# One address difference of activations and weights, modulo 256 bytes, in all products of a two-layer decoder trunk

## The chip, the cores and the metric

The kernel runs on one core of one Trainium2 chip. The metric is the device time of one execution in microseconds (us). The kernel before took 1021.05 us in the median of three runs (1021.05, 1022.01 and 1016.73). One further execution was profiled.

## What is computed

Two decoder layers over 256 tokens with a width of 1024, all in float32. The reference, cut to what matters here:

```python
for layer in range(2):
    if layer == 1:
        k_sh, v_sh, F_sh = shared_kv(x, c_act, ...)      # keys, values, forget gates, once
    sh1, sc1, g1, sh2, sc2, g2, sh3, sc3, g3 = split(c_act @ ada_w[layer] + ada_b[layer], 9)
    h = rms_norm(x, norm_g[layer, 0]) * (1 + sc1) + sh1
    x = x + 0.5 * g1 * swiglu(h, ffn_w_in[layer, 0], ffn_w_out[layer, 0])
    h = rms_norm(x, norm_g[layer, 1]) * (1 + sc2) + sh2
    x = x + g2 * (diff_attention(h, ...) if layer == 0 else forgetting_attention(h, ...))
    h = rms_norm(x, norm_g[layer, 2]) * (1 + sc3) + sh3
    x = x + 0.5 * g3 * swiglu(h, ffn_w_in[layer, 1], ffn_w_out[layer, 1])
return rms_norm(x, final_g)
```

`swiglu(h, w_in, w_out)` is `(silu(g) * u) @ w_out` with `g, u = split(h @ w_in)`; the hidden width is 2816. The four feed-forward networks (FFNs) are named (layer, place) here: (0,0), (0,1), (1,0), (1,1). They hold most of the work.

## The kernel before

**Products.** Activations lie transposed: 8 blocks `k` of 128 channels by 256 tokens. Each float32 operand is split into a high part in the format fp32r and the rest, and a product is made of three matmuls, `wh*xh`, `wl*xh` and `wh*xl` (`mm3`, line 391). Each has a 128x128 block of weights as its stationary operand, which is loaded with an instruction of its own, and 256 columns of activations as its moving operand (258 in the stages called "late", below). Each weight load runs beside the matmul ahead of it. In the products with the values' weights (`v_proj`) the roles are exchanged.

**Where the operands lie.** `HH` and `HL` (lines 399 and 400) hold the high and low parts of the normed activations, 8 blocks of `SP_` = 288 columns, 1152 bytes apart. `hidh` and `hidl` hold those of the hidden layer of an FFN, 512 columns each. Weights come in pieces of up to 1024 columns: `raw` from HBM, `wh` made of it by ScalarE (ACT; `cp_part`, line 281), and `wl` by VectorE (DVE; `sub_part`, line 291), in pools of 6, 6 and 5 buffers. Blocks within a piece are 512 bytes apart.

**Stages.** An FFN has input products into PSUM tiles `pg` and `pu` (gate and up; `pf` in the first stage of FFN (0,0), `lg` and `lu` in the first stage of (0,1) and (1,1)), eleven groups `j` of 96 matmuls, `k` the outer loop in each, and then output products into `po`, 8 tiles of 66 matmuls. Between the FFNs stand the differential attention (0) with its output projection `pw`, the shared keys and values, and the forgetting attention (1). A stage is called "late" where its first products run on activations that are not yet divided by their root mean square: that factor `r` comes from a matmul `psn` with a matrix of equal entries over the sum of squares `acc` (all but the last) and the last square `sq` (`rstd_of`, line 441), while the products `lp` or `lg` run on; then `make_h` (line 456) writes the true `HH` and `HL` block by block with a buffer `ht` between its three steps (DVE, ACT, DVE). The shared keys begin so: `lp` for the first two tiles of keys (`late_pairs`, line 491), then `pk` for the others, from the new `HH` and `HL`, then `pzf`, the forget gates, from weights `fg`, which ACT and DVE split into `fgh` and `fgl` (lines 986 to 999).

**What sets the order.** Instructions of TensorE (PE), ACT, DVE and the DMA queue of SyncE (SP) stay in the order in which the program names them; a planner (`InOrder`, `fill_act`, `fill_dve`, `bg`) puts the conversions of weights between the others by costs of its own. Instructions that the program gives directly to GpSimd (POOL), the DMA of `fg` among them, are placed by the scheduler of the tile framework. A tile with a tag takes the next buffer of its pool's tag and has to wait until the last reader of the tile that held it is done.

Of the kernel before, what the change touches and what calls it, by code (L numbers as in the profile page):

```python
# [10 lines left out]
F32 = mybir.dt.float32  # L11
F32R = mybir.dt.float32r
# [20 lines left out]
SX = S + 2  # L33
SP_ = 288
CP_SLACK = 0.3
# [71 lines left out]
def trunk(ctx, tc, a, out):  # L107
# [45 lines left out]
    cact = cp_.tile([P, D], F32, name="cact")  # L153
    small = cp_.tile([P, 32], F32, name="small")
    nmods = [0]
# [82 lines left out]
    def add_ffn(l, i):  # L238
        if (l, i) == (0, 0):
# [18 lines left out]
    pieces = [(src, c0, min(step, ncols - c0), c0 + step >= ncols)  # L258
              for src, ncols, step in stream for c0 in range(0, ncols, step)]
    raws, his, los = [], [], []  # L260
    taken = [0]
# [19 lines left out]
    def cp_part():  # L281

        u = len(his)
        n = pieces[u][2]
        act.t = max(act.t, used[u - NHI] if u >= NHI else 0.0)
        raw = raws[u]
        wh = wp.tile([P, 1024], F32R, tag="wh", name="wh")
        act.plainly(lambda: act.copy(wh[:, :n], raw[:, :n]))
        his.append(wh)

    def sub_part():
# [5 lines left out]
        dve.t = max(dve.t, used[u - NLO] if u >= NLO else 0.0)  # L297
        wl = wp.tile([P, 1024], F32R, tag="wl", name="wl", bufs=NLO)
        dve.plainly(lambda: dve.tensor_tensor(wl[:, :n], raws[u][:, :n], his[u][:, :n].bitcast(F32),
# [112 lines left out]
    def x_update(n, ps, gate, nxt, acc_eng):  # L412
# [14 lines left out]
        def second():  # L427
# [5 lines left out]
            elif n < NC - 1:  # L433
                t = kp.tile([P, S], F32, tag="acc", name=f"acc{n}")
                acc_eng.tensor_tensor(t, acc[0], sq, op=ALU.add)
# [20 lines left out]
    def make_h(k, r, m):  # L456

        A, sh = mods[m[0]][1], mods[m[1]][0]
        t = kp.tile([P, S], F32, tag="ht", name=f"ht{k}", bufs=3)
        dve.scalar_tensor_tensor(t, x[k], A[:, k:k + 1], r, op0=ALU.mult, op1=ALU.mult)  # L460
# [30 lines left out]
    def late_pairs(src, dsts, m, then):  # L491
# [5 lines left out]
        def out(i):  # L497
            c = late_cols(pb[i])
            for b in range(2):
                t = kp.tile([P, S], F32, tag="lt", name="lt")  # L500
                dve.tensor_tensor(t, pb[i][b][:, :S], r, op=ALU.mult)
# [23 lines left out]
    def ffn(l, i, kind, m, nxt, at=2):  # L525
# [56 lines left out]
        elif kind == "late":  # L582
# [19 lines left out]
            def late_out(b):  # L602
                if b == 0:
                    cols.append(late_cols(banks))
                c = cols[0]
                t = kp.tile([P, S], F32, tag="lt", name=f"lt{b}")
                dve.tensor_tensor(t, banks[b][:, :S], r, op=ALU.mult)
# [377 lines left out]
    vb = [[cp_.tile([P, 512], F32, name=f"vb{t}{nh}") for nh in range(2)] for t in range(2)]  # L985
    fg = kp.tile([P, NC, BH], F32, tag="fg", name="fg", bufs=1)
    nc.gpsimd.dma_start(fg, a["fgw"])
# [313 lines left out]
```

## Time and profile before

| | |
|---|---|
| runs, median (lowest to highest) | 1021.05 us (1016.73 to 1022.01) |
| profiled execution, its own time | 1017.31 us |
| its span in the trace | 1015.4 us |
| PE, matmuls | 991.7 us busy, 8076 matmuls |
| PE, weight loads | 953.8 us busy |
| DVE | 820.2 us busy |
| ACT | 563.5 us busy |
| DMA | 265.06 MB, 261 GB/s in the mean |

The span runs from the first to the last instruction of the program; 1.9 us of the execution's own time lie around it. Matmuls are pipelined: the busy time of one overlaps the next, so the pace of a stream of matmuls is read from start to start, not from the duration of one.

### The profile page before, as it was taken

The page shows a single profiled execution, that of the slowest core. Times are in us where ns is not written, and L with a number is a line of the kernel's source. Part 1 is how long each engine was busy: PE and PEld are TensorE (multiplying, and loading weights), DVE is VectorE, ACT ScalarE, POOL GpSimd, SP SyncE. Part 2 cuts the span into 40 slices and gives each one's busy share as a digit, 9 for nine tenths or more (in the row PEclk, how much of TensorE's full clock was granted, in tenths as well). Part 3 has the DMA queues.
Part 4 walks back from the last instruction along what each step waited for, and adds up shares of the span by engine and source line. Part 5 has one row for each costly group of instructions (what it writes and reads, how often), then busy time and mean ns, then how long its engine had stood idle before and what let it go on. Part 6 is the DMA issues. An engine that isn't in the chain of part 4 may idle for free.

```text
span 1015.4 us, 20397 instructions
## 1 busy us (share of the span) xinstructions
PE 991.7 (98%) x8076; PEld 953.8 (94%) x8076; DVE 820.2 (81%) x1379; ACT 563.5 (55%) x922; POOL 38.1 (4%) x64
## 2 busy tenths in 40 slices
PE   5999999999999999999999999999999999999996
PEld 4999999988899999999998999999987799999996
DVE  6989879899889998878898888889887788555553
ACT  4365545576777645455666444454575575444552
POOL 0000100001111000000000000000011010000000
PEclk9999999999999999999999999999999999999999
DMA  9988999969666799788867999888854337655661
GB/s 348 415 323 281 328 364 340 349 213 339 189 218 214 261 382 338 277 278 309 303 241 262 339 322 349 316 287 323 265 150 124 104 126 238 193 190 148 170 184 42
DMA packets 68129, 265.06 MB, mean 261 GB/s; under 512 B 7961, under 2 KB 8113, under 8 KB 57922
## 3 DMA queue, kind: packets, MB, share of 16 engines
q1 hardware_dynamic: 65810, 258.31, 72.4%
q0 software_dynamic: 1792, 4.81, 1.8%
q8 instruction: 63, 1.03, 0.4%
q10 hardware_dynamic: 432, 0.64, 0.2%
q14 instruction: 32, 0.26, 0.1%
HBM read 262.66 MB, written 2.65 MB: 261 GB/s over the span
## 4 chain that ended last, share of the span: by engine, by line
PE 90%; ACT 3%; DMA 2%; DVE 2%; issue 1%; POOL 1%; SPq 0%; DVEq 0%; ACTq 0%; POOLq 0%
PE po L102 23%; PE pg L102 21%; PE pu L102 21%; PE pf L102 5%; PE pv L102 4%; PE lp L102 3%; PE pw L102 3%; PE pqk L102 1%; ACT nl L102 1%; PE pob L102 1%; PE lg L102 1%; PE lu L102 1%; PE pk L102 1%; PE sb L102 1%; DMA ada<-in_ada 1%
## 5 line engine op out<-in xcount | busy, mean ns | idle before, releaser
L102 DVE TENSOR_TENSOR wl<-raw,wh 128x1024 fp32r<-128x1024 f32 (+1 forms) x368 | 401.7, 1105 | 98.4 <-issue 27.4
L102 ACT CAST wh<-raw 128x1024 fp32r<-128x1024 f32 (+1 forms) x368 | 349.7, 958 | 218.4 <-PE pu L102 107.2
L102 DVE CUSTOM_DVE_ANT_0 ada<-ada,cact,vecs 128x1024 f32<-128x1024 f32 x160 | 203.6, 1279 | 0.0
L102 PE MATMUL po<-hidh,wl 128*128 128x256 f32 x704 | 195.2, 277 | 0.0
L102 PE MATMUL po<-hidl,wh 128*128 128x256 f32 x704 | 195.2, 277 | 0.0
L102 PE MATMUL po<-hidh,wh 128*128 128x256 f32 x704 | 195.2, 277 | 0.0
L102 PE MATMUL pg<-HH,wl 128*128 128x256 f32 x608 | 169.8, 279 | 0.0
L102 PE MATMUL pg<-HH,wh 128*128 128x256 f32 x608 | 169.5, 279 | 0.0
L102 PE MATMUL pg<-HL,wh 128*128 128x256 f32 x608 | 169.4, 279 | 0.0
L102 PE MATMUL pu<-HH,wl 128*128 128x256 f32 x608 | 169.4, 279 | 0.0
L102 PE MATMUL pu<-HH,wh 128*128 128x256 f32 x608 | 169.2, 278 | 0.0
L102 PE MATMUL pu<-HL,wh 128*128 128x256 f32 x608 | 169.2, 278 | 0.0
L102 PEld LDWEIGHTS po<-hidl,wh 128*128 128x128 f32 x704 | 132.9, 189 | 0.0
L102 PEld LDWEIGHTS po<-hidh,wh 128*128 128x128 f32 x704 | 132.2, 188 | 0.0
L102 PEld LDWEIGHTS po<-hidh,wl 128*128 128x128 f32 x704 | 132.2, 188 | 0.0
L102 PEld LDWEIGHTS pg<-HH,wh 128*128 128x128 f32 x608 | 114.2, 188 | 0.7 <-issue 0.6
L102 PEld LDWEIGHTS pu<-HL,wh 128*128 128x128 f32 x608 | 114.4, 188 | 0.0
L102 PEld LDWEIGHTS pg<-HL,wh 128*128 128x128 f32 x608 | 114.2, 188 | 0.0
L102 PEld LDWEIGHTS pu<-HH,wh 128*128 128x128 f32 x608 | 114.2, 188 | 0.0
L102 PEld LDWEIGHTS pg<-HH,wl 128*128 128x128 f32 x608 | 114.1, 188 | 0.0
L102 PEld LDWEIGHTS pu<-HH,wl 128*128 128x128 f32 x608 | 114.1, 188 | 0.0
L102 ACT CAST hidh<-hf 128x512 fp32r<-128x512 f32 x44 | 27.3, 620 | 40.1 <-DVE hf L102 39.9
(204 smaller groups left out, 1603.7 us busy)
## 6 DMA issues: line engine op xcount, KB each, us to landing
raw<-in_win SPq DMA_DIRECT2D x176, 512.0 KB, 5.7
ada<-in_ada SPq DMA_DIRECT2D x79, 1024.0 KB, 7.3
raw<-in_wout SPq DMA_DIRECT2D x64, 384.0 KB, 5.0
raw<-in_wout SPq DMA_DIRECT2D x64, 320.0 KB, 4.4
raw<-in_wqk SPq DMA_DIRECT2D x16, 512.0 KB, 5.9
raw<-in_wo SPq DMA_DIRECT2D x16, 512.0 KB, 4.6
raw<-in_wv SPq DMA_DIRECT2D x8, 512.0 KB, 7.6
raw<-in_wkk SPq DMA_DIRECT2D x8, 512.0 KB, 7.9
```

The source lines that it names most:

```text
L102: return self.tc.keep_in_program_order(f(*args, **kw))
```

## The change

```diff
--- before.py
+++ after.py
@@ -31,7 +31,8 @@
 LAMBDA_INIT = 0.8 - 0.6 * math.exp(-0.3 * 0)
 K0 = 4
 SX = S + 2
-SP_ = 288
+SP_ = 320
+WB = 1088
 CP_SLACK = 0.3
 SUB_SLACK = 0.2
 FULL = 3
@@ -151,7 +152,7 @@
     one = cp_.tile([P, 1], F32, name="one")
     dve.memset(one, 1.0)
     cact = cp_.tile([P, D], F32, name="cact")
-    small = cp_.tile([P, 32], F32, name="small")
+    small = cp_.tile([P, 24], F32, name="small")
     nmods = [0]
     modall = cp_.tile([P, 33, NC], F32, name="modall")
 
@@ -257,6 +258,12 @@
 
     pieces = [(src, c0, min(step, ncols - c0), c0 + step >= ncols)
               for src, ncols, step in stream for c0 in range(0, ncols, step)]
+
+    shift = {}
+    for (l, i), j, count in ((0, 1), 1, 1), ((1, 0), 0, 2), ((1, 1), 1, 3):
+        first = next(p for p, v in enumerate(pieces) if v[0].tensor is a["win"].tensor
+                     and v[0].offset == a["win"][win0_of(l, i) + 2 * j].offset)
+        shift.update({first + p: 16 for p in range(count)})
     raws, his, los = [], [], []
     taken = [0]
     begun = [0]
@@ -284,7 +291,7 @@
         n = pieces[u][2]
         act.t = max(act.t, used[u - NHI] if u >= NHI else 0.0)
         raw = raws[u]
-        wh = wp.tile([P, 1024], F32R, tag="wh", name="wh")
+        wh = wp.tile([P, WB], F32R, tag="wh", name="wh")[:, shift.get(u, 0):]
         act.plainly(lambda: act.copy(wh[:, :n], raw[:, :n]))
         his.append(wh)
 
@@ -295,7 +302,7 @@
             return
         n = pieces[u][2]
         dve.t = max(dve.t, used[u - NLO] if u >= NLO else 0.0)
-        wl = wp.tile([P, 1024], F32R, tag="wl", name="wl", bufs=NLO)
+        wl = wp.tile([P, WB], F32R, tag="wl", name="wl", bufs=NLO)[:, shift.get(u, 0):]
         dve.plainly(lambda: dve.tensor_tensor(wl[:, :n], raws[u][:, :n], his[u][:, :n].bitcast(F32),
                                               op=ALU.subtract))
         los.append(wl)
@@ -431,7 +438,7 @@
             if n == 0:
                 acc[0] = sq
             elif n < NC - 1:
-                t = kp.tile([P, S], F32, tag="acc", name=f"acc{n}")
+                t = kp.tile([P, S], F32, tag="acc", name="acc", bufs=1) if n == 1 else acc[0]
                 acc_eng.tensor_tensor(t, acc[0], sq, op=ALU.add)
                 acc[0] = t
             else:
@@ -456,7 +463,7 @@
     def make_h(k, r, m):
 
         A, sh = mods[m[0]][1], mods[m[1]][0]
-        t = kp.tile([P, S], F32, tag="ht", name=f"ht{k}", bufs=3)
+        t = kp.tile([P, S], F32, tag="ht", name=f"ht{k}")
         dve.scalar_tensor_tensor(t, x[k], A[:, k:k + 1], r, op0=ALU.mult, op1=ALU.mult)
         hh, hl = hn[k]
         act.activation(hh, t, AF.Identity, bias=sh[:, k:k + 1])
@@ -497,7 +504,7 @@
         def out(i):
             c = late_cols(pb[i])
             for b in range(2):
-                t = kp.tile([P, S], F32, tag="lt", name="lt")
+                t = kp.tile([P, S], F32, tag="sq", name="lt")
                 dve.tensor_tensor(t, pb[i][b][:, :S], r, op=ALU.mult)
                 act.activation(dsts[i][:, b * S:(b + 1) * S], t, AF.Identity, bias=c[:, b:b + 1])
 
@@ -603,7 +610,7 @@
                 if b == 0:
                     cols.append(late_cols(banks))
                 c = cols[0]
-                t = kp.tile([P, S], F32, tag="lt", name=f"lt{b}")
+                t = kp.tile([P, S], F32, tag="sq", name=f"lt{b}")
                 dve.tensor_tensor(t, banks[b][:, :S], r, op=ALU.mult)
                 cs = slice((b % 2) * S, (b % 2) * S + S)
                 if b < 2:
@@ -983,7 +990,7 @@
 
     kT = [cp_.tile([P, 512], F32, name=f"kT{j}") for j in range(4)]
     vb = [[cp_.tile([P, 512], F32, name=f"vb{t}{nh}") for nh in range(2)] for t in range(2)]
-    fg = kp.tile([P, NC, BH], F32, tag="fg", name="fg", bufs=1)
+    fg = kp.tile([P, NC, BH], F32, tag="acc", name="fg", bufs=1)
     nc.gpsimd.dma_start(fg, a["fgw"])
     fb = cp_.tile([BH, 1], F32, name="fb")
     nc.gpsimd.dma_start(fb, a["fgb"])
```

`SP_` becomes 320, so that the blocks of `HH` and `HL` stand 1280 bytes apart, and `small` shrinks by 32 bytes. The buffers of `wh` and `wl` get 1088 columns; a piece listed in `shift` begins 16 columns (64 bytes) into its buffer. Listed are the first piece of the FFN (0,1) from group `j` = 1, the first two pieces of (1,0) from `j` = 0 and the first three of (1,1) from `j` = 1, with 24 matmuls to a piece. The rest makes room in the pool `kp`: `ht` has two buffers where it had three, `acc` is one buffer that is added to in place, `lt` shares the two buffers of `sq`, and `fg` takes the buffer of `acc`.

Where the tiles begin in a partition, in bytes modulo 256, and the difference of weights less activations in a product:

| | before | after |
|---|---|---|
| `HH`, `HL`, even k / odd k | 32 / 160 | 0 / 0 |
| `hidh`, `hidl`, and the attention's outputs in the same buffers | 32 | 0 |
| `wh`, `wl` (pieces in `shift`) | 96 | 64 (128) |
| difference, `HH` or `HL`, even k / odd k | 64 / 192 | 64 / 64 (128) |
| difference, `hidh`, `hidl`, attention's outputs | 64 | 64 |
| difference in `pzf`, even k / odd k | 0 / 128 | 0 / 0 |

The order of the instructions on PE, ACT, DVE and SP is the same. On POOL one moves. Here are the rows of POOL at the program's start and, further down, ahead of the shared keys, before; `fg` and `fb` are the forget gates' weights and bias, `udram` and `skew` belong to the first attention's bias.

```order
L1292 MEMSET const-uint8-127 128x1
L1296 UNCONDITIONAL_BRANCH [waits barrier_Pool_Activation_PE_DVE_SP_gather]
L987 DMA fg<-in_fgw 128x128
L989 DMA fb<-in_fgb 16x1
L792 DMA udram<-ut 8x383 [waits DVE_49]
L795 DMA skew<-udram 128x383 [waits DMASW2_49]
```

The DMA of `fg` waits for nothing. Now POOL in the changed program, from the last sum of squares of the first attention's output on (`fgh` and `fgl` are cleared here, `fdram` and `fkb` belong to the second attention):

```order
L442 TENSOR_TENSOR acc<-acc,sq_3979 128x256 [waits Activation_49,Pool_49]
L1002 MEMSET fgh_6364 128x512 [waits DVE_49,PE_49]
L1003 MEMSET fgl_6365 128x512 [waits PE_49]
L1002 MEMSET fgh_6370 128x512 [waits DVE_49,PE_49]
L1003 MEMSET fgl_6371 128x512 [waits PE_49]
L994 DMA fg<-in_fgw 128x128 [waits DVE_49,PE_49,Pool_49]
L1047 DMA fdram<-fk 16x256 [waits Activation_49]
```

The DMA of `fg` has moved from the program's start to behind the clearing of `fgh` and `fgl`, and has three waits; the value of its wait for PE is that of the matmul `psn<-acc` of the shared keys, the last reader of the buffer that `fg` now takes. What stands behind the first reader of `fg` on ACT, in the changed program (`r` is the factor above, `wh` are pieces for `pk`):

```order
L103 ACTIVATE HH<-x,modall 128x256 [waits DVE_49]
L103 ACTIVATE sq_6349<-x 128x256
L103 CAST fgh_6364<-fg 128x4x16 [waits DMASW2_49,Pool_49]
L103 CAST fgh_6370<-fg 128x4x16 [waits Pool_49]
L103 CAST wh<-raw 128x1024 [waits DMAHW4_49,PE_49,Activation_49]
L103 ACTIVATE r_6405<-psn,eps 128x256 [waits PE_49]
L103 ACT_TABLE_LOAD
L103 CAST wh<-raw 128x1024 [waits DMAHW5_49,PE_49,Activation_49]
L103 CAST wh<-raw 128x1024 [waits DMAHW6_49,PE_49,Activation_49]
```

These rows stand as before; the first `CAST` of `fgh` waits for the moved DMA (DMASW2), and the square root's `ACTIVATE` of `r` is queued behind it.

## Rows read from the trace of the kernel before

**Rows 1.** From the page: the span, the busy time of TensorE's matmuls (PE) and weight loads (PEld) with the other engines, and the granted clock in 40 slices (9 is 90% or more of full speed).

```profile
span 1015.4 us, 20397 instructions
...
PE 991.7 (98%) x8076; PEld 953.8 (94%) x8076; DVE 820.2 (81%) x1379; ACT 563.5 (55%) x922; POOL 38.1 (4%) x64
...
PEclk9999999999999999999999999999999999999999
```

**Rows 2.** The timeline of PE in the first FFN: start (us), duration (us), engine, line, operation, tiles. From 66.45 on nine products of an even k (difference 64 bytes), from 67.47 on twelve of an odd k (192 bytes), at 68.88 the first of the next even k; the rows between, one matmul each, are left out.

```profile
66.45 0.28 PE L102 MATMUL pg<-HH,wh 128*128 128x256 f32 x1
...
67.47 0.28 PE L102 MATMUL pg<-HH,wh 128*128 128x256 f32 x1
...
68.88 0.28 PE L102 MATMUL pg<-HH,wh 128*128 128x256 f32 x1
```

**Rows 3.** The answer on the tile `po` (output products of the FFNs, difference 64 bytes throughout) in four stretches, those of the FFNs (0,0), (0,1), (1,0) and (1,1) in this order: one of the three kinds of product, count, duration in ns min/median/max, first and last start (us).

```profile
L102 PE MATMUL po<-hidh,wh x176: 276/276/278, 142.1 to 201.6; 128*128 128x256 f32 x176
...
L102 PE MATMUL po<-hidh,wh x176: 276/276/278, 438.7 to 498.2; 128*128 128x256 f32 x176
...
L102 PE MATMUL po<-hidh,wh x176: 277/281/281, 674.2 to 736.0; 128*128 128x256 f32 x176
...
L102 PE MATMUL po<-hidh,wh x176: 276/276/278, 945.3 to 1004.8; 128*128 128x256 f32 x176
```

**Rows 4.** The same for the tile `pg` (input products of the FFNs, difference 64 and 192 bytes in turn) in the same four FFNs.

```profile
L102 PE MATMUL pg<-HH,wh x112: 276/279/386, 63.3 to 141.0; 128*128 128x256 f32 x112
...
L102 PE MATMUL pg<-HH,wh x160: 276/279/282, 327.5 to 437.7; 128*128 128x256 f32 x160
...
L102 PE MATMUL pg<-HH,wh x176: 277/281/282, 549.8 to 673.1; 128*128 128x256 f32 x176
...
L102 PE MATMUL pg<-HH,wh x160: 276/279/282, 834.1 to 944.3; 128*128 128x256 f32 x160
```

**Rows 5.** The groups of PE in three stretches of the output projections of the attentions (299.9 to 304.8, 305.5 to 310.2, 814.5 to 821.4 us), difference 64 bytes in all: one kind of product each, count, busy us, mean ns of one, idle before.

```profile
L102 PE MATMUL pw<-oh,wl 128*128 128x256 f32 x14 | 3.9, 281 | 0.0
...
L102 PE MATMUL pw<-oh,wl 128*128 128x256 f32 x15 | 4.1, 276 | 0.0
...
L102 PE MATMUL pw<-obh,wl 128*128 128x256 f32 x20 | 5.6, 281 | 0.0
```

**Rows 6.** The answer on the tile `pzf` (forget gates; the difference is 0 and 128 bytes in turn): count, duration in ns min/median/max, first and last start.

```profile
L102 PE MATMUL pzf<-HH,fgh x8: 280/281/282, 517.1 to 519.6; 128*128 128x256 f32 x8
```

**Rows 7.** From the page, the costliest group of ScalarE (ACT): busy us, mean ns of one, then the idle time before it and what ended that.

```profile
L102 ACT CAST wh<-raw 128x1024 fp32r<-128x1024 f32 (+1 forms) x368 | 349.7, 958 | 218.4 <-PE pu L102 107.2
```

**Rows 8.** The timeline of ACT at the start of the shared keys' products: start, us, engine, line, operation, tiles, in brackets the idle time before and its releaser.

```profile
500.42 0.38 ACT L102 CAST fgh<-fg 128x64 fp32r<-128x64 f32 x2
...
500.70 1.04 ACT L102 CAST wh<-raw 128x1024 fp32r<-128x1024 f32 x1
...
502.44 0.47 ACT L102 ACTIVATE r<-psn,eps 128x256 f32<-128x256 f32 x1 [0.70 <-PE psn L102]
...
502.94 1.28 ACT L102 ACT_TABLE_LOAD   x1
...
504.23 1.05 ACT L102 CAST wh<-raw 128x1024 fp32r<-128x1024 f32 x1
...
506.06 1.05 ACT L102 CAST wh<-raw 128x1024 fp32r<-128x1024 f32 x1 [0.78 <-ACT wh L102]
...
508.48 0.90 ACT L102 ACTIVATE HH<-ht,modall 128x256 fp32r<-128x256 f32 x2
```

**Rows 9.** The timeline of VectorE (DVE) in the same stretch.

```profile
500.75 0.37 DVE L102 TENSOR_TENSOR fgl<-fg,fgh 128x64 fp32r<-128x64 f32 x2
...
501.29 1.23 DVE L102 TENSOR_TENSOR wl<-raw,wh 128x1024 fp32r<-128x1024 f32 x1 [0.17 <-issue]
...
502.95 0.48 DVE L102 SCALAR_TENSOR_TENSOR ra<-psn,eps,r 128x256 f32<-128x256 f32 x1 [0.44 <-ACT r L102]
...
504.27 1.22 DVE L102 TENSOR_TENSOR wl<-raw,wh 128x1024 fp32r<-128x1024 f32 x1
...
505.96 1.23 DVE L102 TENSOR_TENSOR wl<-raw,wh 128x1024 fp32r<-128x1024 f32 x1 [0.47 <-issue]
...
507.20 0.76 DVE L102 TENSOR_TENSOR lt<-lp,r 128x256 f32<-128x256 f32 x2
...
509.01 0.48 DVE L102 SCALAR_TENSOR_TENSOR HL<-ht,modall,HH 128x256 fp32r<-128x256 f32 x1 [0.26 <-ACT HH L102]
...
514.49 0.48 DVE L102 SCALAR_TENSOR_TENSOR HL<-ht,modall,HH 128x256 fp32r<-128x256 f32 x1 [0.24 <-ACT lcol L102]
```

**Rows 10.** The timeline of PE in the same stretch.

```profile
501.38 0.60 PE L102 MATMUL psn<-acc,ones 128*128 128x256 f32 x2
...
511.79 0.29 PE L102 MATMUL pk<-HL,wh 128*128 128x256 f32 x1
...
517.14 0.28 PE L102 MATMUL pzf<-HH,fgh 128*128 128x256 f32 x1
```

**Rows 11.** From the view of DMA issues: tiles, queue, count, KB each, median us from issue to landing, for the one transfer of `fg`.

```profile
fg<-in_fgw POOLq DMA_DIRECT2D x1, 64.0 KB, 4.5
```

**Rows 12.** The last line of the answers on the tiles `fkb` (16 transfers) and `g` (8 transfers, 128 KB each like `fkb`'s), both issued by GpSimd's queue too: time to landing.

```profile
DMA to landing us min/median/max: 3.1/3.6/5.9
...
DMA to landing us min/median/max: 4.0/5.3/6.9
```

## The prediction

> **What bounds the kernel now.** I read the page first. The matmuls of PE are busy for 991.7 of the span's 1015.4 us, and the granted clock is at 9 tenths or more in all 40 slices [rows 1], so it is at 2.4 GHz and has nothing to give back. The reader should see that only the pace of PE's matmuls, and a stop of PE, can move the time. The costliest group of ACT, the conversions of weights, is idle before its instructions for 218.4 us, and 107.2 of that ends with a matmul of `pu` [rows 7]: the conversions wait for PE to give buffers back, not PE for them. A faster PE is therefore fed.
>
> Then the pace, in the timeline of PE. Nine products of an even k take 67.47 - 66.45 = 1.02 us, 113.3 ns each; twelve of an odd k take 68.88 - 67.47 = 1.41 us, 117.5 ns each [rows 2]. The only thing in which the two differ is where the operands lie. The answers on whole tiles are finer. From the first to the last `po<-hidh,wh` of an FFN there are 175 x 3 = 525 matmuls, and they take 59.5 us in three of the FFNs, 113.3 ns each, but 61.8 us in (1,0), 117.7 ns each [rows 3]. All have a difference of 64 bytes. For the input products I count 951 matmuls from the first to the last `pg<-HH,wh` over ten groups and 1047 over eleven: 110.2 us, 115.9 ns each, in (0,1) and (1,1), and 123.3 us, 117.8 ns each, in (1,0) [rows 4].
>
> So there are two paces, 113.3 and 117.8 ns. With 192 bytes I find the slow one alone. With 64 bytes there are both: a stretch begins in one and keeps it to its end, 525 matmuls in a row in the FFN (1,0). The output projections of the attentions, all at 64 bytes, show the same in short stretches between waits, 276 ns for one matmul in one and 281 in others [rows 5], where 276 goes with the fast pace and 281 with the slow one [rows 3]. The difference of 64 bytes permits the fast pace; it does not ensure it.
>
> **The change, part by part.** *Odd k, 192 to 64 bytes.* If the fast pace holds, each gains 117.8 - 113.3 = 4.45 ns. FFN (0,0) has 528 such products (`pf` and seven groups of `pg` and `pu`, 48 to a group), (0,1) and (1,1) have 480 each: 1488 x 4.45 ns = 6.6 us. The FFN (1,0) is slow throughout, and there all 1056 + 528 products can gain: 1584 x 4.45 ns = 7.05 us. The attentions' and keys' own products with `HH` and 256 columns, 240 at odd k, gain 0.5 us if half of their short stretches are fast. The products with 258 columns I leave at 0; no row shows them at 64 bytes for long.
>
> *Pieces that lie 64 bytes further on.* 24 + 48 + 72 = 144 products get a difference of 128. The nearest row is that of the forget gates, at 0 and 128 in turn, with 281 ns, the duration of the slow pace [rows 6]. So these lose the gain: 144 x 4.45 ns = 0.6 us. What they do to the pace behind them is the open point of this forecast, and the bounds are the two paces: after them an FFN runs fast or slow.
>
> *The pools.* `lt` in the buffers of `sq`, and `acc` in place, add waits for readers that are long done. `ht` with two buffers makes each DVE step wait for the one just ahead of it, which matters only where that chain is late, next. `fg` is what costs. Its DMA stood at the program's start. Now it waits for `psn<-acc` of the shared keys, and behind `fgh` stand, on ACT, the cast for `pk`, `r`, a table load and two casts, and on DVE, behind `fgl`, the whole of the rest. In the trace `psn<-acc` ends at 501.38 + 0.60 = 501.98 [rows 10]. The same transfer took 4.5 us to land [rows 11], so `fg` is there at about 506.5, and `fgh`, which began at 500.42 [rows 8], begins 6.1 us later. From there I follow the two queues:
>
> ACT: two `fgh` 0.38, cast 1.04, so `r` runs from about 507.9 to 508.4; table load 1.28, to 509.7; cast 1.05, to 510.75 [rows 8]. DVE: `fgl` and a `wl` are done by 508.4; three steps to `r`, which took 504.27 - 502.95 = 1.3 us, end at 509.8; `wl` 1.22, to 511.05; the next `wl`, 1.23, to 512.3; `lt` 0.76, to 513.05 [rows 9]. Then the first `HL` starts 509.01 - 507.20 - 0.76 = 1.05 us later, at 514.1 where it was 509.01, and ends at 514.6. The first matmul that reads it started at 511.79 [rows 10], so PE stops for 2.8 us. The last `HL` follows the first by 514.49 - 509.01 = 5.5 us and ends at 520.1. Its reader, the third of the last six matmuls of `pk`, stood four matmuls ahead of the end of `pk` at 517.14 [rows 10], at 516.7: 3.4 us late. With two buffers of `ht` six steps come up to 0.1 us later each (thirteen steps of DVE fill the 5.5 us, 0.42 apart, where one runs 0.48 us: they overlap as long as they do not wait for one another). That makes 4.0 us. Nothing hides it, since PE has no idle time to spend [rows 1]. Bounds: the landings of other transfers from this queue lie between 3.1 and 6.9 us [rows 12], so the loss lies between 2.5 and 6.5 us.
>
> The Trainium skill, in "SBUF — State Buffer", the DMA setup-cost knee, fits a transfer's time as about 2 us plus the bytes over 436 GB/s. For the 64 KB of `fg` that would be an estimate of 2.2 us and a loss of some 1.7 us; the trace shows 4.5 us for this very transfer [rows 11], and the trace decides.
>
> *The sum.* 6.6 + 7.05 + 0.5 - 0.6 - 4.0 = 9.5 us less than the profiled execution's own 1017.31 us (its span and 1.9 us around it): 1007.8, say 1008 us. The median of the runs, 1021.05, is 3.7 us above the profiled execution, and two of three runs are 4.3 to 5.3 us above the third. A FFN with alternating differences that is slow throughout costs (480 + 528) x 4.45 ns = 4.5 us more than one that is half fast; I take the spread to be that, one FFN more in the slow pace. The changed kernel has no such half: with one difference an FFN is all fast or all slow.
>
> **The rivals.** *One FFN falls into the slow pace* and keeps it. It costs 1488 to 1584 x 4.45 ns, so 6.6 to 7.05 us: 1014.8 us. For it: an FFN of the four in the trace is slow at the same 64 bytes. Against it: three are fast.
>
> *Two FFNs slow*: 1021.5 us, no change.
>
> *Three or four slow*: this ends on the other side. Before, the change of the difference at each k breaks a slow stretch, and three FFNs come back to the fast pace at every even k [rows 2, 4]; a constant difference takes that away, and an FFN which is slow after its first group stays so for some 170 us. From the third slow FFN on the kernel is slower: 1028 us, or 1035 with all four. For it: the long slow stretches of [rows 3, 5]. Against it: four of the seven stretches of [rows 3, 5] are fast, and of the FFNs' own three of four.
>
> *The addresses do nothing*, and the two paces come from something that goes with k. Then the loss on `fg` alone is left: 1017.3 + 4.0 = 1021.3 us. The rows speak against it, because `po` has no even and odd k in `HH` and shows both paces. The Trainium skill states the rule that would make it true: "TensorE: Matmul & The Clock Gate", step-by-step, says that matmul and weight load have independent read ports and that loading the next weights takes no read bandwidth from the running matmul. By that no address could matter; 276 against 281 ns for the same operation on the same shapes [rows 3] does not agree.
>
> **How the numbers follow.** All four fast, 1008 us, within 1004 to 1011 by the bounds of the loss: 0.50. One slow, 1013 to 1017: 0.22. Two slow: 0.12. Three or four: 0.08. No effect of addresses: 0.08. About 0.5% is what a measurement of this kernel can tell from no change, which is 1015.9 and 1026.2 us against the median. Faster takes the first case and most of the second, 0.67; slower takes the third and fourth slow FFN, 0.08; the rest is no change, 0.25. For 8 in 10 the range runs from 1004 up through the cases of one and two slow FFNs, to 1021.5; the likeliest case alone is 1004 to 1011.
>
> **What would show it right or wrong.** Right: `po` at 276 ns and 59.5 us in all four FFNs; `pg<-HH,wh` over ten groups in 951 x 113.3 ns = 107.8 us and a little more for the shifted pieces; `fgh` some 6 us after `psn`'s first row's place before, and PE idle for about 3 us ahead of `pk`, ended by `HH` or `HL`. Wrong: any FFN whose `po` shows 281 ns, no stop at `pk`, or `pk` stopped for over 6 us. If `po` is slow in three FFNs, the difference was not what mattered, but how a stretch begins.

## The result and the profile after

The changed kernel takes 1009.61 us (median of 11 runs, 1006.72 to 1015.65), the kernel before 1016.85 us in the same set (11 runs, the three known before among them, 1012.88 to 1022.01). The ratio is 0.993, with a 95% interval of 0.9904 to 0.9956: 0.7% faster. A ratio leaves out runs more than 1.5% above the fastest of their own kernel, which concerns two of the twelve runs of the kernel without shifted pieces, below. The forecast was 1008.0 us. The profiled execution took 1012.33 us, some 3 us above the median, and its trace says why.

From the page of the changed kernel, the span, the busy time and the granted clock in 40 slices, which answer to [rows 1]:

```profile
span 1010.4 us, 20397 instructions
...
PE 986.9 (98%) x8076; PEld 948.1 (94%) x8076; DVE 821.5 (81%) x1379; ACT 562.3 (56%) x922; POOL 38.1 (4%) x64
...
PEclk9999999999999999999999999999999999999999
```

The same number of matmuls, the same granted clock (9 tenths or more everywhere, so 2.4 GHz), and 4.8 us less of busy PE. Now the answers on `po` and then on `pg` in the FFNs (0,0), (0,1), (1,0) and (1,1), which answer to [rows 3] and [rows 4]; columns: count, duration in ns min/median/max, first and last start:

```profile
L103 PE MATMUL po<-hidh,wh x176: 276/276/277, 138.3 to 197.8; 128*128 128x256 f32 x176
...
L103 PE MATMUL po<-hidh,wh x176: 276/276/277, 433.2 to 492.8; 128*128 128x256 f32 x176
...
L103 PE MATMUL po<-hidh,wh x176: 276/276/277, 666.6 to 726.1; 128*128 128x256 f32 x176
...
L103 PE MATMUL po<-hidh,wh x176: 281/281/282, 938.1 to 999.9; 128*128 128x256 f32 x176
...
L103 PE MATMUL pg<-HH,wh x112: 276/276/385, 61.2 to 137.3; 128*128 128x256 f32 x112
...
L103 PE MATMUL pg<-HH,wh x160: 276/276/285, 324.3 to 432.2; 128*128 128x256 f32 x160
...
L103 PE MATMUL pg<-HH,wh x176: 276/276/285, 546.7 to 665.6; 128*128 128x256 f32 x176
...
L103 PE MATMUL pg<-HH,wh x160: 279/281/285, 824.9 to 937.0; 128*128 128x256 f32 x160
```

Three FFNs are now at 276 ns in `pg` too, where before the median was 279, a mixture; the fourth, (1,1), is at 281 from its first `pg` to its last `po`. From the first `pg` to the last `po` the four take 136.6, 168.5, 179.4 and 175.0 us, against 138.3, 170.7, 186.2 and 170.7 us before: -1.7, -2.2, -6.8 and +4.3 us. So this execution is the forecast's rival in which one FFN is slow.

The stop on `fg`, in the timelines of GpSimd, ScalarE, VectorE and TensorE (start, us, engine, operation, in brackets the idle time before it and what ended it), which answers to [rows 8], [rows 9] and [rows 10]:

```profile
496.41 0.58 POOL L994 DMA_DIRECT2D fg<-in_fgw  x1 [8.08 <-PE psn L103]
...
499.36 0.39 ACT L103 CAST fgh<-fg 128x64 fp32r<-128x64 f32 x2 [4.74 <-DMA fg<-in_fgw]
...
499.70 0.38 DVE L103 TENSOR_TENSOR fgl<-fg,fgh 128x64 fp32r<-128x64 f32 x2 [4.86 <-ACT fgh L103]
...
495.25 0.59 PE L103 MATMUL psn<-acc,ones 128*128 128x256 f32 x2
...
506.79 0.39 PE L103 MATMUL pk<-HH,wh 128*128 128x256 f32 x1 [1.07 <-ACT HH L103]
...
514.11 0.28 PE L103 MATMUL pzf<-HH,fgh 128*128 128x256 f32 x1
```

The chain is the one that was forecast: the DMA waits for `psn`, the cast for the DMA, and at its end PE is idle for 1.07 us ahead of `pk`, whose products then follow the late `HH` and `HL` one by one (7.2 us from the first to the last of the 48, 5.5 us before). From `psn` to `pzf` it takes 18.86 us, where it took 517.14 - 501.38 = 15.76 us [rows 10]: 3.1 us.

The FFNs sum to -6.4 us and `fg` to +3.1. The first `pg` stands 2.1 us earlier (61.2 against 63.3 us), which is mostly the start ahead of the first product, `pf`: it stands at 14.70 us, before at 16.47. Over the profiles of all runs here it lies between 14.70 and 17.47 us, and in the second profile of the changed kernel at 15.34, so this belongs to the execution and not to the change. Some 0.4 us lost in the rest close the difference of the spans, 5.0 us.

### The profile page after: what moved, and what is told of

It is laid out like the page before. It is cut to its first block, busy times and chain, and to the rows that moved or that the text cites. A ratio compares the mean times of both kernels' runs of the same rounds, so it can differ in the third digit from the quotient of the medians.

```text
span 1010.4 us, 20397 instructions
## 1 busy us (share of the span) xinstructions
PE 986.9 (98%) x8076; PEld 948.1 (94%) x8076; DVE 821.5 (81%) x1379; ACT 562.3 (56%) x922; POOL 38.1 (4%) x64
## 4 chain that ended last, share of the span: by engine, by line
PE 91%; ACT 4%; DVE 3%; issue 1%; POOL 1%; DMA 0%; SPq 0%; DVEq 0%; ACTq 0%
PE po L103 24%; PE pg L103 21%; PE pu L103 21%; PE pf L103 5%; PE pv L103 4%; PE pw L103 3%; PE lp L103 3%; PE pk L103 1%; ACT nl L103 1%; PE pob L103 1%; PE lg L103 1%; PE lu L103 1%; PE pqk L103 1%; PE sb L103 1%; ACT on L103 1%; DVE ada L103 1%
```

## The experiments

Two theories stood against each other. The prediction's: the difference of the addresses sets the pace; 192 bytes are slow, 64 bytes may be fast, and the shifted pieces cost their own 144 products. Its rival: the paces come from how a stretch begins, and the shifted pieces act on what comes behind them. No kernel here leaves out any of the computation. A mean pace below is the mean time from the start of one matmul to the start of the next in the trace, without the waits.

**The DMA of `fg` early.** `fg` lies in a buffer of a tile that is written only later, so its DMA stands at the program's start again:

```diff
-    fg = kp.tile([P, NC, BH], F32, tag="acc", name="fg", bufs=1)
+    fg = vb[1][1][:, :NC * BH].rearrange("p (k b) -> p k b", b=BH)
```

> The changed kernel, but the forget gates' weights `fg` lie in a buffer of their own, and their DMA stands at the program's start again, as before the change. Theory (the later DMA of `fg` holds up `fgh`, the casts behind it and `pk`): PE's stop ahead of `pk` of the shared keys goes, `pzf` starts 2 to 4 us earlier against `psn` (15.8 us after it, as before the change, where the changed kernel has 18.9), and the median is about 3 us below the changed kernel's 1009.6: 1006.6 us. Rival (the stop comes from `ht` with two buffers or from the sums in place): the stop stays, and the time is 1009.6 us. Each FFN still shows one of the two paces, 113.3 or 117.8 ns from matmul to matmul, and the spread of the runs stays.

1006.15 us (6 runs, 1004.09 to 1011.02), 0.9902 of the kernel before (0.9868 to 0.9936). In its PE timeline:

```profile
498.13 0.59 PE L103 MATMUL psn<-acc,ones 128*128 128x256 f32 x2
...
513.87 0.28 PE L103 MATMUL pzf<-HH,fgh 128*128 128x256 f32 x1
```

15.74 us, as before the change, with no idle time ahead of `pk`. `ht` still has two buffers here, and the sums stay in place: where `fg` is early, these edits cost nothing that can be seen. All four FFNs are at 276 ns in this profile. The interval of the time overlaps that of the changed kernel (0.9904 to 0.9956); it is the trace that shows the stop gone.

**The pools alone.** The kernel before, with the pool edits of the change and none of its addresses:

```diff
-                t = kp.tile([P, S], F32, tag="acc", name=f"acc{n}")
+                t = kp.tile([P, S], F32, tag="acc", name="acc", bufs=1) if n == 1 else acc[0]
...
-        t = kp.tile([P, S], F32, tag="ht", name=f"ht{k}", bufs=3)
+        t = kp.tile([P, S], F32, tag="ht", name=f"ht{k}")
...
-    fg = kp.tile([P, NC, BH], F32, tag="fg", name="fg", bufs=1)
+    fg = kp.tile([P, NC, BH], F32, tag="acc", name="fg", bufs=1)
```

> The kernel before with the edits of the pools alone: `ht` with two buffers, the sums in place, `lt` in the buffers of `sq`, `fg` in the buffer of the sums; no address of activations or weights moves. Theory (these edits cost the stop ahead of `pk` and nothing else): 2.5 to 4 us above the kernel before, 1.003 to 1.004 of it, with `pzf` 18.9 us after `psn`, not 15.8. Rival (the stop is hidden or is due to the changed pace): no difference, 1.000. The gain of the addresses alone is then the measured gain of 7.2 us plus what this costs.

1020.11 us (12 runs), 1.0038 (1.0008 to 1.0067): 3.9 us slower, as the theory had it. The stop is there, 520.09 - 500.69 = 19.40 us from `psn` to `pzf`:

```profile
500.69 0.60 PE L102 MATMUL psn<-acc,ones 128*128 128x256 f32 x2
...
520.09 0.28 PE L102 MATMUL pzf<-HH,fgh 128*128 128x256 f32 x1
```

The profile also shows something of the kernel before. The FFN (1,0), slow throughout in its trace [rows 3], is not slow here, at the same differences; its `po`:

```profile
L102 PE MATMUL po<-hidh,wh x176: 276/276/278, 675.1 to 734.6; 128*128 128x256 f32 x176
```

**No shifted pieces.** All weights at 64 bytes:

```diff
-    for (l, i), j, count in ((0, 1), 1, 1), ((1, 0), 0, 2), ((1, 1), 1, 3):
+    for (l, i), j, count in ():
```

> The changed kernel without the shift of the first weight parts: all weights and activations lie 64 bytes apart. Theory (a stretch keeps the pace that it began with, and the pieces at 128 bytes end a slow one): FFN (1,0), whose first group is now at 64 bytes too, runs slow in some or all executions, as it did before the change, and (0,1) and (1,1) may; some 6.6 to 7 us for each, so 1013 to 1023 us. Rival (the shifted pieces only cost their own 144 products at the slow pace): 0.6 us less than the changed kernel, 1009.0 us, with the same FFNs fast and slow.

1019.56 us (12 runs, 1012.37 to 1033.33), 1.0037 (1.0005 to 1.007): slower than the kernel before. In the profiled execution (1018.53 us) two FFNs are slow from end to end, (0,1) and (1,1), while (1,0), which the theory had first in mind, is fast; the answer on `po`:

```profile
L103 PE MATMUL po<-hidh,wh x176: 276/276/276, 138.9 to 198.4; 128*128 128x256 f32 x176
...
L103 PE MATMUL po<-hidh,wh x176: 281/281/281, 438.0 to 499.8; 128*128 128x256 f32 x176
...
L103 PE MATMUL po<-hidh,wh x176: 276/276/276, 672.6 to 732.1; 128*128 128x256 f32 x176
...
L103 PE MATMUL po<-hidh,wh x176: 281/281/281, 944.1 to 1005.9; 128*128 128x256 f32 x176
```

The twelve runs lie in heaps: 1012.4; six of 1018.5 to 1019.9; three of 1024.5 to 1026.4; 1030.6 and 1033.3. The steps are those of one FFN (6.6 to 7.05 us). Only a run of the second heap was profiled, with two slow FFNs; that the others are one, three and four is worked out from the steps. So the constant difference by itself is worth nothing: its 1.0037 is the 1.0038 of the pools. The mean of all twelve runs, 1022.3 us, is 1.0056 of the mean before. The 144 products that were shifted bring the rest: 1.0037 - 0.993 = 1.07%, 10.9 us, or some 13 us with all twelve runs, between two sets of runs.

**A scan of differences.** With `fg` early, every group of `pg` and `pu` and every tile of `po` has a difference of its own (the columns by which a group's pieces are shifted, 4 bytes each):

```diff
+    order = {(0, 1): (1, [0, 8, 16, 24, 32, 40, 48, 56, 0, 8]),
+             (1, 0): (0, [56, 48, 40, 32, 24, 16, 8, 0, 32, 0, 16]),
+             (1, 1): (1, [32, 0, 48, 16, 56, 24, 40, 8, 16, 0])}
...
+    out0 = {(0, 0): [0, 8, 16, 24, 32, 40, 48, 56], (0, 1): [0, 56, 48, 40, 32, 24, 16, 8],
+            (1, 0): [0, 4, 12, 20, 28, 36, 44, 52], (1, 1): [0, 16, 48, 0, 4, 60, 2, 62]}
```

> A look at the pace as a function of the difference alone: the weights of each group of `pg` and `pu` and of each tile of `po` in the FFNs lie at a difference of their own, from 64 to 64 + 252 bytes modulo 256, in steps of 16 or 32 bytes; `fg` is early as in the run with the early DMA. Theory (the address difference modulo 256 bytes sets which paces are possible): 113.3 ns in some of the differences near 64 bytes, 117 to 119 ns at 0, 128 and 192, and the same difference gives the same paces wherever it stands in the program, up to the two paces at 64. Rival (a stretch is fast or slow by how it begins, whatever the addresses): the pace does not follow the difference, and whole FFNs are fast or slow. The time is between 1008 and 1030 us.

1031.24 us in one execution. Mean paces, by stretches of 66 or 96 products (in brackets: once):

```
difference, bytes      0      32     64              96             128    160    192    224
pace, ns               119.9  118.3  113.4 or 117.8  117.3 (118.7)  118.7  119.9  117.8  116.7 or 117.9
```

0, 32, 128, 160 and 192 each have one pace wherever they stand (0 gave 119.85 to 120.00 in six places), so the rival "whatever the addresses" falls. But 64, 96 and 224 had two. At 64 the pace went with what stood ahead: behind 192 or 128 fast, behind 0 and 32 slow. Behind 96 it was slow once, in (1,0) at 638.5 us, and fast once, in (0,1) at 446.4 us; the next expectation has 96 as always slow, which is a misreading.

**Short stretches at other differences.** Two kernels with stretches of 18 to 96 products at 128, 192 or 0 inside the FFNs, 64 elsewhere (shift in columns, pieces; from the first kernel, both lists cut short):

```diff
+    kicks = {(0, 0, 1): (16, 1), (0, 0, 3): (16, 2), (0, 0, 5): (16, 3), (0, 1, 0): (32, 4), (0, 1, 2): (16, 1),
...
+    outs = {(0, 0, 1): (16, 1), (0, 0, 3): (16, 2), (0, 0, 5): (48, 4), (0, 1, 1): (48, 4), (0, 1, 3): (16, 4),
```

> The run with the early DMA of `fg`, but the shifted pieces are others: stretches of 15 to 96 products at 128, 192 or 0 bytes lie inside the FFNs, one every two groups of `pg` and `pu` or every two tiles of `po`, and 64 bytes elsewhere. In the run without shifted pieces the pace at 64 bytes held to the end of an FFN; in the scan 64 bytes was fast after 192 or 128 and slow after 0, 32 and 96. Theory (the pace at 64 bytes is decided where the stretch begins, by the pace ahead of it and by the number and the difference of the products between, and then holds): the pace at 64 changes only at these stretches, never inside one; equal stretches with an equal pace ahead have the same outcome; fast after 192, slow after 96 products at 0. Rival (the pace at 64 changes by chance or by what the other engines do): changes also where no piece is shifted, and equal stretches with unequal outcomes. The time is between 1008 and 1025 us.

> As the run with stretches at other differences inside the FFNs, with other numbers and another order of them, so that the same stretch (24 products at 128, 24 and 96 at 192, 96 at 0) is met after a fast and after a slow stretch at 64. Theory: the same outcome as in the run before for the same stretch and the same pace ahead; rival: other outcomes. The time is between 1008 and 1025 us.

1019.32 and 1023.59 us, one execution each. In the second the seven stretches from 950 us, the answer on `po` of FFN (1,1), show how it goes at 0, 64 and 192. Their differences are 64, 192, 64, 0, 64, 192 and 64 bytes:

```profile
L103 PE MATMUL po<-hidh,wh x22: 276/276/276, 950.2 to 957.4; 128*128 128x256 f32 x22
...
L103 PE MATMUL po<-hidh,wh x11: 276/276/276, 957.7 to 961.1; 128*128 128x256 f32 x11
...
L103 PE MATMUL po<-hidh,wh x33: 276/276/276, 961.5 to 972.3; 128*128 128x256 f32 x33
...
L103 PE MATMUL po<-hidh,wh x22: 283/283/283, 972.7 to 980.2; 128*128 128x256 f32 x22
...
L103 PE MATMUL po<-hidh,wh x22: 281/281/281, 980.6 to 988.0; 128*128 128x256 f32 x22
...
L103 PE MATMUL po<-hidh,wh x22: 278/280/280, 988.4 to 995.8; 128*128 128x256 f32 x22
...
L103 PE MATMUL po<-hidh,wh x22: 276/276/277, 996.1 to 1003.3; 128*128 128x256 f32 x22
```

Fast at 64 stays fast through 192 (and 192 itself is fast there); 0 turns it slow; slow at 64 is slow at 192 too, and behind that 64 is fast again. Over both kernels: 64 behind 0 was slow in 26 of 26 cases, behind 192 fast in 8 of 8, behind 128 fast in 9 of 9 where the stretch ahead was fast, and in 12 of 12 where it was slow, except with just 24 products at 128 (1 of 4). Between such stretches the pace at 64 changed only in FFN (0,0), at a product that started late (222 ns behind the one ahead, at 56.8 us, in the second kernel). One step of the expectation fell: equal stretches of 24 products at 128, each behind a slow one, had unequal outcomes, so the pace ahead does not say everything; the last section has what the traces show of it.

**192 or 0 at the head of the FFNs.** With `fg` early, 24 products at the head of each FFN, and 24 more inside (0,0), at 192 bytes or at 0; with 192 the late first groups `lg` and `lu` too:

```diff
-    for (l, i), j, count in ((0, 1), 1, 1), ((1, 0), 0, 2), ((1, 1), 1, 3):
+    for (l, i), j, count in ((0, 0), 0, 1), ((0, 0), 5, 1), ((0, 1), 0, 5), ((1, 0), 0, 1), ((1, 1), 0, 5):
...
-        shift.update({first + p: 16 for p in range(count)})
+        shift.update({first + p: 32 for p in range(count)})
```

> The run with the early DMA of `fg`, with other shifted pieces: 24 products at 192 bytes (128 further on than the others) at the head of each FFN and once more behind the wait inside FFN (0,0), and the weights of the late first groups (`lg`, `lu`) at 192 too; nothing lies at 128. In the two looks, every stretch at 192 of 18 to 96 products was followed by the fast pace at 64. Theory (what a FFN does is decided by the stretch at its head): all four FFNs are at 113.3 ns in the profile, and in nearly all executions, so the runs lie closer together than those of the changed kernel, 1003.5 to 1007 us, median 1004.5 to 1005.5 us, under the 1006.15 us of the run with the early DMA. Rival (the head of an FFN makes the fast pace likelier only): runs some 6.6 us apart as before, median 1006 us or more.

```diff
-    for (l, i), j, count in ((0, 1), 1, 1), ((1, 0), 0, 2), ((1, 1), 1, 3):
+    for (l, i), j, count in ((0, 0), 0, 1), ((0, 0), 5, 1), ((0, 1), 1, 1), ((1, 0), 0, 1), ((1, 1), 1, 1):
...
-        shift.update({first + p: 16 for p in range(count)})
+        shift.update({first + p: 48 for p in range(count)})
```

> The same, with the 24 products at the head of each FFN at 0 bytes instead (192 further on than the others), and `lg` at 64; 120 products of some 8900 differ from the run without any shifted piece. In the two looks every stretch at 0 was followed by the slow pace at 64. Theory: all four FFNs are at 117.8 ns to their ends. That is 1200 products in (0,0), 1488 in (0,1) and in (1,1) and 1584 in (1,0), 5760 x 4.45 ns = 25.6 us above four fast FFNs (1004 to 1006 us): 1030 to 1032 us, slower than the kernel before by 1.4%. Rival (the paces are a matter of chance that shifted pieces only disturb): the paces of the run without shifted pieces, some 1016 us, since `fg` is early.

With 192: 1004.23 us (6 runs), 0.9867 (0.9831 to 0.9903), and all four FFNs at 276 ns in the profile from behind the 24 products on. Their `po`:

```profile
L103 PE MATMUL po<-hidh,wh x176: 276/276/276, 139.7 to 199.2; 128*128 128x256 f32 x176
...
L103 PE MATMUL po<-hidh,wh x176: 276/276/276, 434.4 to 493.9; 128*128 128x256 f32 x176
...
L103 PE MATMUL po<-hidh,wh x176: 276/276/276, 664.5 to 724.0; 128*128 128x256 f32 x176
...
L103 PE MATMUL po<-hidh,wh x176: 276/276/276, 931.6 to 991.1; 128*128 128x256 f32 x176
```

Five runs lie within 2.5 us (1002.97 to 1005.46); a sixth at 1012.34 has no trace and stays unexplained, so the rival that such a head only makes the fast pace likelier is not excluded. With 0: 1029.70 us (6 runs, 1028.62 to 1030.97), 1.0102 (1.007 to 1.0133), and `po` of its four FFNs:

```profile
L103 PE MATMUL po<-hidh,wh x176: 281/281/281, 144.2 to 206.1; 128*128 128x256 f32 x176
...
L103 PE MATMUL po<-hidh,wh x176: 281/281/281, 445.7 to 507.5; 128*128 128x256 f32 x176
...
L103 PE MATMUL po<-hidh,wh x176: 281/281/281, 682.8 to 744.6; 128*128 128x256 f32 x176
...
L103 PE MATMUL po<-hidh,wh x176: 281/281/281, 956.5 to 1018.3; 128*128 128x256 f32 x176
```

The two differ by 25.5 us, where 5760 x 4.45 ns = 25.6 us was expected. The heads decide what thousands of products behind them take; (1,0), which has no `lg`, shows it with its 24 products alone. One stretch went another way: in (0,0) 72 products at 64, behind a wait that ended at 113.3 us, ran fast until the second 24 at 0.

**The changed kernel again.**

> The changed kernel itself once more. Theory (72 products at 128 bytes at the head of FFN (1,1) leave it fast in some executions and slow in others): the runs lie in two heaps some 6.6 us apart, near 1007 and 1013.5 us, median between 1007 and 1012 us; in the profile some FFN that starts behind late products may be slow, from its head to its end. Rival (FFN (1,1) is slow in every execution of this program, and the spread comes from elsewhere): (1,1) slow again and one heap.

1007.69 us (6 runs), 0.99 (0.9865 to 0.9935). Together with the eleven of the first set, 10 of 17 runs lie between 1005.95 and 1009.61 us and 7 between 1011.15 and 1015.65. In this profile (1012.41 us) it is FFN (0,0) that is slow, and (1,1), with the same 72 products at 128 at its head, is fast. Their `po`:

```profile
L103 PE MATMUL po<-hidh,wh x176: 281/281/281, 142.8 to 204.6; 128*128 128x256 f32 x176
...
L103 PE MATMUL po<-hidh,wh x176: 276/276/276, 940.5 to 1000.0; 128*128 128x256 f32 x176
```

(0,0) has no shifted piece in this kernel. In the first profile its pace changed at late products alone: slow behind one that started 226 ns after the one ahead, at 50.4 us, and fast again behind the next such product, at 56.1 us.

**All weights at 192, and parts at 64 and 192 in turn.** With `fg` early; first everything at 192 with 24 products at 64 at the heads, then every second part at 192:

```diff
-    shift = {}
+    shift = {p: 32 for p in range(len(pieces))}
...
-        shift.update({first + p: 16 for p in range(count)})
+        shift.update({first + p: 0 for p in range(count)})
```

> The run with the early DMA of `fg`, with all weights at 192 bytes instead of 64; only 24 products at the head of each FFN (and behind the wait in (0,0)) lie at 64. In the two looks and in the run with 192 at the heads, products at 192 behind a fast stretch at 64 took 113.3 ns, behind a slow one 117.7. Theory (192 bytes have both paces as 64 have; what made every product of an odd k slow in the kernel before is that its activations alternate between two places modulo 256, and not the number 192): whole FFNs at 192 run at 113.3 ns where the 24 products at 64 came out fast, and the time is 1003 to 1012 us. Rival, the prediction's own reading (192 permits the slow pace alone): 117.8 ns in all FFNs, 5800 products x 4.45 ns = 26 us above the best run, 1029 us and more.

```diff
-    shift = {}
-    for (l, i), j, count in ((0, 1), 1, 1), ((1, 0), 0, 2), ((1, 1), 1, 3):
...
+    shift = {p: 32 * (p % 2) for p in range(len(pieces))}
```

> The run with the early DMA of `fg`, with every second weight part at 192 bytes and the others at 64, so that the difference changes every 24 products (18 and 15 in `po`) by the weights' address, the activations' staying the same. Theory (192 behind slow products leads to the fast pace and 192 behind fast ones keeps it): from the second part on every FFN is fast, at 64 and at 192, and the time is 1003 to 1007 us. Rival (a difference that alternates makes the products at 192 slow, whichever operand moves): 113.3 ns at 64 and 117.6 at 192, 115.5 on the mean, some 13 us above that: 1016 to 1019 us.

All at 192: 1006.49 us (6 runs), 0.9883 (0.9861 to 0.9904). All FFNs but (0,0) are fast at 192 to their ends, here `pg` and `po` of (0,1):

```profile
L103 PE MATMUL pg<-HH,wh x160: 276/276/285, 328.2 to 436.0; 128*128 128x256 f32 x160
...
L103 PE MATMUL po<-hidh,wh x176: 276/276/276, 437.0 to 496.5; 128*128 128x256 f32 x176
```

So 192 bytes permit the fast pace as 64 do. FFN (0,0) is slow up to 120.7 us, where the second 24 products at 64 turn it fast; the first 24, at 63.2 us, did not, with 370 slow products at 192 ahead of them. Among the kernels with moved weights that is the one case against "fast behind 192" without a late product between. In turn: 1004.58 us in one execution. In three FFNs both differences take 113.3 ns from the second part of `pg` on; in (0,0) there are slow parts from 46.8 to 58.3 us and near 111 us, each stretch of them behind a product that started late, and at the next 64 behind 192 the fast pace comes back each time. That kernel was then timed:

> The kernel whose weight parts lie at 64 and 192 bytes in turn, once more and timed. Theory (a slow stretch is ended by the next part at 192, wherever it began, so no FFN can stay slow): the runs lie within 3 us, 1003.5 to 1006.5 us, median 1004.6 us, and none is 6 us above the others. Rival (the alternation only makes the fast pace likelier): one or more of the runs at 1010 us or above.

1003.16 us (6 runs, 1002.75 to 1003.95), 0.9849 (0.98 to 0.9898). It has the lowest median here, and its runs lie within 1.2 us of one another. Its page and its last `po`:

```profile
PE 978.1 (98%) x8076; PEld 940.1 (94%) x8076; DVE 821.4 (82%) x1379; ACT 561.5 (56%) x922; POOL 37.9 (4%) x64
...
L103 PE MATMUL po<-hidh,wh x176: 276/276/277, 931.9 to 991.4; 128*128 128x256 f32 x176
```

## Why the prediction came out right, and where its reasons did not

*What bounds the kernel* held: PE's pace and a stop of PE moved the time, in every run.

*Odd k, 6.6 and 7.05 us*: the sizes are right. `pg` over ten groups took 107.9 us in (0,1), as forecast; (1,0) gained 6.8 us. But some 4.4 us of these belong to the one execution that was profiled before, in which (1,0) was slow throughout (186.2 us); with the same differences it was half fast in the kernel with the pools alone, from 552.8 to 734.6 us, 181.8 us. And the reason given, that 192 bytes have the slow pace alone, is wrong: whole FFNs run fast at 192. What makes the odd k slow in the kernel before is not settled. There the activations' address alternates, every 6 or 12 products; in the last kernel the weights' address alternates, every 15 to 24, and both differences are fast. In the trace before, a stretch at 192 bytes is at 118 ns from its first interval on, so its own length cannot be the reason. Whether it is the operand that moves, or the few products at 64 ahead, was not tried.

*The shifted pieces, -0.6 us*: this is the step that failed. Their own price was near (118.7 ns, 144 x 5.4 ns = 0.8 us). What they do to the pace behind them was named as the open point, and it proved to be the change's whole gain: without them the kernel is at 1.0037, with them at 0.993. The sum took the gain at odd k for the work of the constant difference and the shifted pieces for a loss. The rivals of two and of three or four slow FFNs are what the constant difference does without them: by their heaps six and five of the twelve runs.

*All four fast* was given 0.50 and *one FFN slow* 0.22. Of the 17 runs 10 lie in the first case's 1004 to 1011 us; the other 7 begin at 1011.15, three of them under the 1013 of the second case, and two of these three are the profiled ones, with one slow FFN each. So both profiles show a sign that the prediction had set for being wrong, an FFN whose `po` is at 281 ns. That the spread of the runs is whole FFNs is borne out by the heaps. That an FFN *keeps* its pace does not hold everywhere: in (0,0) it changed at late products.

*The wait for `fg`, 4.0 us*: 3.1 us in the trace, 3.5 us between the medians of two sets with and without it, 3.9 us with the pools alone. The place and the queue behind it are as forecast; the idle time ahead of `pk` is there, but 1.07 us and not some 3, the rest being lost between the products of `pk`. Mis-sized was the landing: `fg` arrived 499.36 - 496.41 = 2.95 us after its issue, not 4.5 us [rows 11]. The Trainium skill, "SBUF — State Buffer", the DMA setup-cost knee, by which 2.2 us was an estimate, came nearer to this landing than the one row before (0.75 us too short, that one 1.5 us too long). The loss of 1.7 us that went with it is 1.4 us too low, the forecast's 4.0 us 0.9 us too high.

*The attentions and the products with 258 columns*, +0.5 and 0: from the first `lp` to the first `pg` behind it, the two attentions took 0.6 and 0.8 us longer than before. Part of it are the 258-column products: at 64 they take 120.9 ns, where half at 64 and half at 192 took 119.6 on the mean, 460 x 1.3 ns = 0.6 us lost in all of them.

*The addresses do nothing* is excluded: 120 products at 0, against the same 120 and the 192 of the late groups at 192, move the time by 25.5 us. The Trainium skill, "TensorE: Matmul & The Clock Gate", step-by-step, has loading the next weights take no read bandwidth from the running matmul. If that were all there is, the heads at 192 and at 0 would give one time; these runs do not agree with it.

The number came out because these errors are small and of both signs: a slow FFN in some runs and the loss in the attentions, against a cheaper `fg`. Luck has its part in it. The sum starts from one profiled execution, 1017.31 us, which happens to lie near the median of a kernel whose runs here spread from 1011.42 to 1024.92 us. And the median of the changed kernel, 1009.61 us, is the highest of the 6 runs of 11 in the lower heap; with one run more in the upper heap it would have been 1011.15 us.

## What to carry to other kernels

Where PE is the bound and the same shape shows two durations (here 276 and 281 ns) in long unbroken stretches, ask how each stretch begins, not only what its addresses are: a few dozen products at another difference can set the pace of the next 1500. Make the fast pace come back by itself, with weights at two differences in turn, rather than count on a good start; with `fg` early it gave 1.5% against the kernel before, in runs within 1.2 us, where the pieces of the change gave 1.0% with `fg` early (the intervals, 0.98 to 0.9898 and 0.9868 to 0.9936, still touch). And price a buffer that is shared to make room by the queue behind its first reader: `fg` cost 3 to 4 us for a transfer of 64 KB.

## What the runs showed of the hardware that was not expected

The pace of back-to-back products depends on the difference of the two addresses modulo 256 (113.3 to 119.9 ns on the mean) and on history: at 64 and at 192 bytes there are two steady paces, 113.3 and 117.8 ns, and the slow one lasted through all 1584 products of (1,0) in the kernel before. The experiments move the weights alone; that it is the difference rests on the kernel before, where weights at 96 run at 113.3 ns beside activations at 32, while in the scan weights at 96 beside activations at 0 took 117.3 ns.

In the two kernels with short stretches, 0 left 64 slow 26 times of 26 and 192 left it fast 8 times of 8, with one case against the latter in another kernel. Against it stands also the kernel before, where the activations move and not the weights: in its (1,0), 64 came behind 192 at 43 even k and stayed slow at every one. So it is for moved weights that 192 was seen to bring the fast pace back.

At 128 the single intervals run through a cycle of five (122, 120, 119, 115, 118 ns), and where in it a stretch ends differs between executions. The pace behind it goes with that place. In six of the traces 64 follows 128 inside an FFN at 36 places: the 4 that ended on the interval behind the 115 were slow, the 32 that ended elsewhere fast. Among them are both outcomes at the head of (1,1) in the changed kernel: where the FFN was slow, its 72 products ended there, and where it was fast, an interval earlier. No run chose the place itself, so that it is the cause is likely, but not shown.
